# A hybrid decoder layer: the loads behind the weight sums, one token sum's place, and the queue of one transfer

## The chip, the cores and the metric

The kernel runs on one NeuronCore of one Trainium2 chip. Its engines are TensorE (PE in the profile, with PEld for its weight loads), VectorE (DVE), ScalarE (ACT), GpSimd (POOL) and SyncE (SP). The metric is the device time of one execution in microseconds (us). It is compared with the kernel before on the same chip.

## The reference

One layer (DEPTH = 1) works on 256 tokens of width 2048, in float32:

```python
h = rmsnorm(x, norm_mix_g)
u = h @ w_in                       # 2048 x 16384: c, b, xa, za, q, f, iv, og, ga, gb
ya = b * causal_dwconv3(c * xa, conv_w) * silu(za)
yb = per-head rmsnorm(chunked gated recurrence of q, f, iv) * hg_norm_g * silu(og)
m = sigmoid(ga) * (ya @ w_a_out) + sigmoid(gb) * (yb @ w_b_out)
x = x + m @ w_o
gate = sigmoid(rmsnorm(x, ple_norm_g) @ w_ple_gate)
x = x + gate * (p @ w_ple_proj)
out = rmsnorm(x, final_norm_g)
```

## The kernel before, in words

**Three products for one.** Each float32 operand of a large matmul is cut into a high part, which ScalarE writes (`cut`, L169, tiles named ...hi), and a low part, which VectorE writes as the rest (L170, ...lo). TensorE then multiplies three times into the same PSUM bank: high with high (L1038), low with high (L1039), high with low (L1040). The weights come in as raw tiles, `raw[128, 2, 1024]`, which SyncE's queue loads one MB at a time into three buffers (`load`, L150). Each holds two items. One item is 256 rows of the weight matrix by 512 columns and costs twelve matmuls of 128x512; its high and low parts have four buffers.

**The order of the work.** A list `items` gives all items in order, and the loop over `pos` walks through it. At each position it cuts the item three places ahead, multiplies the item at hand, starts loads up to four further ahead, and advances generators (`active`) that hold the epilogues: each `yield` in an epilogue is one position of the loop. The instructions of each engine then stand in an order that a scheduler settles, apart from a stretch (`pinned`) where the traced order is kept. Every queue and engine works its own instructions in order, so one that waits holds up those behind it.

**Seven products for eight.** For the groups j = 1, 2, 3 of the gates ga and gb, five of the eight items (`SEVEN`, c = 0, 2, 3, 5, 6, kind "S") are done with seven block products in place of eight. This needs sums of weight blocks and sums of token blocks. `token_sums` makes the sums of token blocks once, four for each such c (s1 to s4), cuts them and keeps them as `shi`, `slo` in the pool `st`. `combine_weights` makes the sums of weight blocks for each of the fifteen units, two positions ahead. It takes three tiles: `sA` and `sB`, plain loads on SyncE's queue in two buffers each, and `sT`, in three buffers. `sT` is itself a sum, built by two transfers on GpSimd's queue (`add_by_dma`): a plain load (L157), then a second transfer that adds two more blocks to it on its way in (L163). The second waits until the first has landed. The first three pairs are issued at positions fixed by `begun`; every later pair is issued when a unit has been combined. `unit_products` does the seven products of a unit; the block product with the weights `bhi`, `blo` (one buffer) goes third.

**The merged quarters.** `ep_bb` (L778 on) merges the two branches to one quarter of m, 128x1024. Three quarters wait in DRAM. The last one (j = 3) is turned at once: `turned` writes it to DRAM in four transfers (L304), reads it back with another (L315) on SyncE's queue, lets `lag` positions pass, transposes it on VectorE (L308, `back<-t`) and cuts it (`put_m`: L775 on ScalarE, L776 on VectorE) into the operand `mh`, `ml` of the product with `w_o`. That product needs the last quarter only from its seventh item on. The scheduler has put the first item of the next group of columns ahead of this seventh item.

Lines of the steps below: L141 loads of sA and sB; L150 raw loads; L157 and L163 the two transfers of sT; L169 and L170 the cuts; L701 the sums of weights; L760, L762, L763 the sums of tokens and their cut; L308, L315, L775, L776 the way back of the last quarter; L993 and L997 loads of x for the residual and of the final gain.

Of the kernel before, what the change touches and what calls it, by code (L numbers as in the profile page):

```python
# [9 lines left out]
F32 = mybir.dt.float32  # L10
F32R = mybir.dt.float32r
AF = mybir.ActivationFunctionType
ALU = mybir.AluOpType
PSUM = bass.MemoryType.PSUM

P = 128
# [7 lines left out]
CW = 512  # L24
# [7 lines left out]
SEVEN = [()] + 3 * [(0, 2, 3, 5, 6)]  # L32
# [15 lines left out]
def hybrid_kernel(ctx, tc, xT, x, pT, prm, gfin, masks, w_in, w_a, w_b, w_o, w_pg, w_pp, out):  # L48
    nc = tc.nc
# [9 lines left out]
    pools, closers = {}, {}  # L59
# [13 lines left out]
    state = {"tmp": "tmp1"}  # L73
# [3 lines left out]
    def nm(s):  # L77
        uid[0] += 1
        return f"{s}_{uid[0]}"
# [16 lines left out]
    pair_sums = {}  # L96
# [9 lines left out]
    items = []  # L106
# [16 lines left out]
    def raw_of(pos):  # L123
        it = items[pos]
        if it["raw"] not in loaded:
            if it["kind"] == "S":
                t = tuple(
                    pools["st"].tile([P, n, CW], F32, tag=tag, bufs=2, name=nm(tag)) for tag, n in (("sA", 2), ("sB", 1))
                )
            else:  # L130
                t = wp.tile([P, 2, 2 * CW], F32, tag="raw", bufs=3, name=nm("raw"))
            loaded[it["raw"]] = t
        return loaded[it["raw"]]
# [18 lines left out]
    def add_by_dma(behind=None):  # L152
        pos = next((n for n, it in enumerate(items) if it["kind"] == "S" and n not in pair_sums), None)
        if pos is not None:
            w, g, c = items[pos]["w"]
            X = pair_sums[pos] = pools["st"].tile([P, 2, CW], F32, tag="sT", bufs=3, name=nm("sT"))
            d = nc.gpsimd.dma_start(out=X.rearrange("p n x -> p (n x)"), in_=w[g + 1, :, c, :])  # L157
            if behind is not None:
                tc.add_manual_dep(
                    d.ins, behind.name,  # L160
                    mybir.DependencyInfo(mybir.DependencyClass.Sync, mybir.DependencyReason.DATA), reason="order",
                )
            nc.gpsimd.dma_start(out=X, in_=w[g : g + 2, :, c, :CW].rearrange("n p x -> p n x"), accum_op=ALU.add)  # L163

    def pair_of(pool, n, tags=("whi", "wlo"), width=2 * CW):
        return tuple(pool.tile([P, width], F32R, tag=tag, bufs=n, name=nm(tag)) for tag in tags)
# [18 lines left out]
    def combine_weights(pos):  # L185
        st = pools["st"]
        (A, B), X = raw_of(pos), pair_sums[pos]
        add(A[:, 0], X[:, 0], B[:, 0])
        add(A[:, 1], A[:, 0], A[:, 1])
        ts = []  # L190
        for n, src in enumerate((X, B, A)):
            hi, lo = pair_of(st, 1, ("bhi", "blo"), CW) if n == 1 else pair_of(st, 3, ("thi", "tlo"))
# [9 lines left out]
    begun = next(n for n, it in enumerate(items) if it["kind"] == "ga" and it["last"])  # L202
# [7 lines left out]
    prm_t = const.tile([P, PRM_N], F32, name="prm_t")  # L210
    praw = pools["tmp1"].tile([P, 1024], F32, tag="X", bufs=4, name="praw")[:, : 2 * T]
    pop = pools["tmp1"].tile([P, 1024], F32R, tag="X", bufs=4, name="pop")
# [87 lines left out]
    def to_dram(src, tag, bufs):  # L300
        d = dram.tile([P, 4, T], F32, tag=tag, bufs=bufs, name=nm(tag))
        to = d.rearrange("(b i) a x -> a i b x", b=4)
        for a in range(4):
            nc.sync.dma_start(out=to[a], in_=src[32 * a : 32 * a + 32, :].rearrange("i (b x) -> i b x", b=4))  # L304
        return d

    def square_turn(dst, src):
        nc.vector.transpose(  # L308
            out=dst.rearrange("p (k a e) -> p a k e", a=4, e=32), in_=src.rearrange("p (a k e) -> p a k e", a=4, e=32)
        )  # L310

    def turned(src, lag, dst=None):
        d = to_dram(src, "turn", 3)
        yield
        nc.sync.dma_start(out=src, in_=d.rearrange("p a x -> p (a x)"))  # L315
        for _ in range(lag):
            yield
        dst = t4() if dst is None else dst
        square_turn(dst, src)
        return dst  # L320
# [379 lines left out]
    def add(out, a, b):  # L700
        nc.vector.tensor_tensor(out=out, in0=a, in1=b, op=ALU.add)  # L701
# [32 lines left out]

    def token_sums():
        nu = len(SEVEN[1])
        state["S"] = pair_of(pools["st"], 1, ("shi", "slo"), nu * 4 * P)
        state["S"] = tuple(v.rearrange("p (u s t) -> p u s t", u=nu, s=4) for v in state["S"])
        yield
        yield  # L740
        for first, n in TOGETHER:
            yield
            F, S = (
                pools["st"].tile([P, 2 * CW], F32R, tag=tag, bufs=3, name=nm(tag))[:, : n * 4 * P].bitcast(F32)
                for tag in ("thi", "tlo")
            )
            c = SEVEN[1][first]
            hi, lo = (v[:, 2 * c : 2 * (c + n), :] for v in state["hT"])
            Fv = F.rearrange("p (k t) -> p k t", t=T)
            nc.vector.tensor_tensor(out=Fv, in0=hi.bitcast(F32), in1=lo.bitcast(F32), op=ALU.add)  # L750
            yield
            Fv = F.rearrange("p (u r b t) -> p u r b t", u=n, r=2, b=2)
            Sv = S.rearrange("p (u s t) -> p u s t", u=n, s=4)
            a11, a12, a21, a22 = Fv[:, :, 0, 0], Fv[:, :, 1, 0], Fv[:, :, 0, 1], Fv[:, :, 1, 1]
            s1, s2, s3, s4 = (Sv[:, :, i] for i in range(4))
            for out, u, v, op in (
                (s1, a21, a22, ALU.subtract), (s2, s1, a11, ALU.subtract),
                (s3, a11, a21, ALU.subtract), (s4, a12, s2, ALU.add),
            ):
                nc.vector.tensor_tensor(out=out, in0=u, in1=v, op=op)  # L760
            hi, lo = (v[:, first : first + n] for v in state["S"])
            nc.scalar.activation(out=hi, in_=Sv, func=AF.Copy)  # L762
            nc.vector.tensor_tensor(out=lo, in0=Sv, in1=hi.bitcast(F32), op=ALU.subtract)  # L763
            yield

    def ep_a(j, psum):
# [11 lines left out]
    def ep_bb(j, psum):  # L778
        ga, gb = state["ga"], state["gb"]
        for t in range(NT):  # L780
            s = slice(t * CW, (t + 1) * CW)
            nc.vector.tensor_tensor(out=gb[:, s], in0=gb[:, s], in1=psum[t], op=ALU.mult)
        m = t4()
        for t in range(NT):
            s = slice(t * CW, (t + 1) * CW)
            nc.vector.tensor_tensor(out=spread(m, t), in0=blocks(ga[:, s]), in1=blocks(gb[:, s]), op=ALU.add)
        if j == 3:
            m = yield from turned(m, 3, back())
            put_m(j, m)
        else:  # L790
            state["m", j] = to_dram(m, f"m{j}", 1)
            yield

    def back():
        return pools["back"].tile([P, 1024], F32, tag="back", bufs=5, name=nm("back"))
# [259 lines left out]
    def names_of(it):  # L1055
        if it["kind"] == "C":
            return [("c", it["n"], t) for i in range(2) for t in range(NT)]
        return ["P1", ("c", 0, 0), ("c", 1, 0), "P5", "P7", "P6", ("c", 0, 1)]

    def into(name, op, part):  # L1060
        left[name] -= 1
# [3 lines left out]
    def unit_products(pos):  # L1065
        it = items[pos]
        c, h = it["c"], state["hT"]

        def x_of(r, t):
            return tuple(v[:, 2 * c + r, t * P : (t + 1) * P] for v in h)  # L1070

        hi, lo = parts.pop(pos)
        halves = [(hi[:, i * CW : (i + 1) * CW], lo[:, i * CW : (i + 1) * CW]) for i in range(2)]
        names = names_of(it)
        if it["kind"] == "C":
            for n, name in enumerate(names):
                into(name, x_of(n // 2, n % 2), halves[n // 2])
            return
        b22, t1, t3, t2, t4_ = sums.pop(pos)
        s1, s2, s3, s4 = (tuple(v[:, SEVEN[1].index(c), i] for v in state["S"]) for i in range(4))  # L1080
        for name, op, part in zip(names, (x_of(0, 0), x_of(1, 0), s4, s1, s3, s2, x_of(1, 1)),
                                  (halves[0], halves[1], b22, t1, t3, t2, t4_)):
            into(name, op, part)

    def pinned(start):
# [16 lines left out]
    for pos, it in enumerate(items[:last_group]):  # L1102
        mark = len(nc.cur_bb.bb.instructions)
        kind, j, c, last = (it[n] for n in ("kind", "j", "c", "last"))
        _, _, w, g, opname = groups[it["gi"]]
# [60 lines left out]
        else:  # L1166
            if c == 0:
                psum = [bank("s" if kind == "PP" and j >= 2 else "g") for _ in range(NT)]
            hi, lo = parts.pop(pos)
            for i in range(2):  # L1170
                k = 2 * c + i
                s = slice(i * CW, (i + 1) * CW)
# [10 lines left out]
        if pos == begun:  # L1183
            finish()
            second_part()
            active.append(token_sums())
        if pos in (begun + 3, begun + 5, begun + 7):
            add_by_dma(state["splits"][0])
        if kind == "O" and j == 0 and c == nch - 3:
            finish()  # L1190
# [23 lines left out]
    for t, halves in ((0, (0, 1)), (1, (0,)), (1, (1,))):  # L1214
        bk, n = bank("g"), CW // 2
        for c in range(nlast):
# [3 lines left out]
            hi, lo = parts[last_group + c]  # L1220
            for i in range(2):
                k = 2 * c + i
                s = slice(i * CW + halves[0] * n, i * CW + (halves[-1] + 1) * n)
# [83 lines left out]
```

## Time and profile before

| | |
|---|---|
| time, median of 3 runs (lowest to highest) | 817.6 us (816.24 to 818.68) |
| the profiled execution: time, span | 816.5 us, 814.7 us |
| granted TensorE clock | 0.996 of full speed |
| busy: PE, PEld, DVE, ACT, POOL | 803.2, 665.4, 589.2, 459.4, 48.5 us |
| moved by DMA | 198.52 MB, mean 244 GB/s |

The span runs from the first instruction to the last. The time of an execution holds the span and what lies around it, here 1.8 us. All positions below, such as "at 473.0", are us from the start of the span.

### The profile page before, as it was taken

The numbers are of one execution on the slowest core, as the hardware profiler recorded it, in microseconds if no ns is written. First come the engines' busy times: TensorE is split into PE (matmuls) and PEld (weight loads), VectorE is DVE, ScalarE is ACT, GpSimd is POOL, SyncE is SP. The second block draws the span as 40 slices with busy tenths as digits, with TensorE's granted clock in tenths as the row PEclk, the third lists the DMA queues.
The fourth block names the chain that finished last, engine by engine and source line by source line (L and its number), as shares of the span: only waits on it lengthen the run. The fifth ranks groups of instructions, "written<-read, shape, count | busy, mean of one in ns | idle before, by whom it ended". The sixth has DMA issues, their size and how long they took to land.

```text
span 814.7 us, 10651 instructions
## 1 busy us (share of the span) xinstructions
PE 803.2 (99%) x4059; PEld 665.4 (82%) x4059; DVE 589.2 (72%) x745; ACT 459.4 (56%) x614; POOL 48.5 (6%) x57
## 2 busy tenths in 40 slices
PE   9999999999999999999999999999999999999995
PEld 6888888888888888888888878888888788888885
DVE  7746588767766498767679968987988756677932
ACT  7576476466565466456455546556554546566623
POOL 1000000001000000010011110110100000001210
PEclk9999999999999999999999999999999999999998
DMA  9988555648867555648789989998944888777802
GB/s 339 392 307 288 197 201 175 233 139 267 252 237 249 198 175 196 207 157 269 259 296 282 286 268 297 284 280 260 283 163 177 291 300 300 255 274 298 276 34 103
DMA packets 52659, 198.52 MB, mean 244 GB/s; under 512 B 6784, under 2 KB 16256, under 8 KB 37888
## 3 DMA queue, kind: packets, MB, share of 16 engines
q1 hardware_dynamic: 45504, 180.54, 63.6%
q0 software_dynamic: 6240, 15.73, 8.2%
q10 hardware_dynamic: 864, 1.57, 0.5%
q8 instruction: 31, 0.51, 0.2%
q14 instruction: 20, 0.16, 0.1%
HBM read 184.19 MB, written 13.63 MB: 243 GB/s over the span
## 4 chain that ended last, share of the span: by engine, by line
PE 85%; DVE 7%; issue 4%; DMA 2%; ACT 2%; POOL 0%; POOLq 0%; DVEq 0%; ACTq 0%
PE g L1038 26%; PE g L1039 26%; PE g L1040 25%; DVE wlo L170 3%; PE s L1039 2%; PE s L1040 2%; PE s L1038 2%; DMA sT<-in_w_in 1%; DMA raw<-in_w_o 1%; PE s L484 1%; DVE sA L701 1%; ACT whi L169 0%; DVE tlo L170 0%; PE s L932 0%; DVE back L308 0%
## 5 line engine op out<-in xcount | busy, mean ns | idle before, releaser
L170 DVE TENSOR_TENSOR wlo<-raw,whi 128x1024 fp32r<-128x1024 f32 (+1 forms) x264 | 319.9, 1229 | 159.9 <-ACT whi L169 158.0
L169 ACT ACTIVATE whi<-raw 128x1024 fp32r<-128x1024 f32 (+1 forms) x264 | 272.9, 1051 | 208.1 <-PE g L1040 175.2
L1038 PE MATMUL g<-whi,xh 128*128 128x512 f32 (+1 forms) x738 | 283.8, 385 | 0.0
L1039 PE MATMUL g<-wlo,xh 128*128 128x512 f32 (+1 forms) x738 | 283.7, 384 | 0.0
L1040 PE MATMUL g<-whi,xl 128*128 128x512 f32 (+1 forms) x738 | 283.6, 384 | 0.0
L1040 PEld LDWEIGHTS g<-whi,xl 128*128 128x128 f32 x738 | 138.7, 188 | 27.8
L1038 PEld LDWEIGHTS g<-whi,xh 128*128 128x128 f32 x738 | 138.7, 188 | 27.5
L1039 PEld LDWEIGHTS g<-wlo,xh 128*128 128x128 f32 x738 | 138.7, 188 | 27.1
L1039 PE MATMUL g<-wlo,mh 128*128 128x512 f32 x128 | 49.9, 390 | 0.3 <-DVE wlo L170 0.3
L1038 PE MATMUL g<-whi,mh 128*128 128x512 f32 x128 | 49.6, 389 | 0.0
L1040 PE MATMUL g<-whi,ml 128*128 128x512 f32 x128 | 49.5, 389 | 0.0
L1040 PE MATMUL s<-whi,xl 128*128 128x512 f32 x84 | 32.7, 389 | 0.0
L1038 PE MATMUL s<-whi,xh 128*128 128x512 f32 x84 | 32.7, 389 | 0.0
L1039 PE MATMUL s<-wlo,xh 128*128 128x512 f32 x84 | 32.7, 389 | 0.0
L169 ACT ACTIVATE thi<-sA 128x1024 fp32r<-128x1024 f32 x15 | 15.9, 1063 | 25.0 <-DVE sA L701 21.3
L1039 PEld LDWEIGHTS g<-wlo,mh 128*128 128x128 f32 x128 | 24.0, 188 | 5.6 <-DVE wlo L170 0.7
L1038 PEld LDWEIGHTS g<-whi,mh 128*128 128x128 f32 x128 | 24.0, 188 | 5.1
L1040 PEld LDWEIGHTS g<-whi,ml 128*128 128x128 f32 x128 | 24.0, 188 | 5.0
L1039 PE MATMUL g<-wlo,ybTh 128*128 128x512 f32 x64 | 24.9, 389 | 0.0
L1040 PE MATMUL g<-whi,ybTl 128*128 128x512 f32 x64 | 24.9, 389 | 0.0
L1038 PE MATMUL g<-whi,yaTh 128*128 128x512 f32 x64 | 24.9, 389 | 0.0
L1039 PE MATMUL g<-wlo,yaTh 128*128 128x512 f32 x64 | 24.9, 389 | 0.0
(215 smaller groups left out, 910.2 us busy)
## 6 DMA issues: line engine op xcount, KB each, us to landing
raw<-in_w_in SPq DMA_DIRECT2D x66, 1024.0 KB, 5.0
raw<-in_w_o SPq DMA_DIRECT2D x16, 1024.0 KB, 6.1
raw<-in_w_pg SPq DMA_DIRECT2D x16, 1024.0 KB, 5.7
sT<-in_w_in POOLq DMA_DIRECT2D x30, 512.0 KB, 8.5
raw<-in_w_in SPq DMA_DIRECT2D x28, 512.0 KB, 6.9
raw<-in_w_a SPq DMA_DIRECT2D x8, 1024.0 KB, 6.4
raw<-in_w_b SPq DMA_DIRECT2D x8, 1024.0 KB, 7.7
turn<-t SPq DMA_DIRECT2D x60, 128.0 KB, 2.8
```

Of the source, the lines that this page charges most:

```text
L169: a = nc.scalar.activation(out=hi, in_=src, func=AF.Copy)
L170: v = nc.vector.tensor_tensor(out=lo, in0=src, in1=hi.bitcast(F32), op=ALU.subtract)
L484: nc.tensor.matmul(out, X[:, 0, h, s], X[:, 1, h, t], start=True, stop=True, tile_position=(0, i * n))
L701: nc.vector.tensor_tensor(out=out, in0=a, in1=b, op=ALU.add)
L1038: nc.tensor.matmul(psum, oh, hi, start=first, stop=False)
L1039: nc.tensor.matmul(psum, oh, lo, start=False, stop=False)
L1040: nc.tensor.matmul(psum, ol, hi, start=False, stop=last)
```

## The change

`sT` gets a fourth buffer and `sB` a third. The plain load of a unit's `sT` is now issued before the accumulating transfer of the unit before it, and a fourth call starts the series, so plain loads run one unit further ahead. Of the four token sums, the fourth (s4) no longer stands in `shi`, `slo`: it takes the place of a block of x that no later product reads, in `xh`, `xl`. Each of the three cuts of token sums becomes two for this, and the product that uses s4 (with `bhi`, `blo`) goes first in its unit instead of third. The last merged quarter is read back on GpSimd's queue, with a lag of 5.

```diff
-                    pools["st"].tile([P, n, CW], F32, tag=tag, bufs=2, name=nm(tag)) for tag, n in (("sA", 2), ("sB", 1))
+                    pools["st"].tile([P, n, CW], F32, tag=tag, bufs=bufs, name=nm(tag))
+                    for tag, n, bufs in (("sA", 2, 2), ("sB", 1, 3))
...
-            X = pair_sums[pos] = pools["st"].tile([P, 2, CW], F32, tag="sT", bufs=3, name=nm("sT"))
+            X = pair_sums[pos] = pools["st"].tile([P, 2, CW], F32, tag="sT", bufs=4, name=nm("sT"))
             d = nc.gpsimd.dma_start(out=X.rearrange("p n x -> p (n x)"), in_=w[g + 1, :, c, :])
...
-            nc.gpsimd.dma_start(out=X, in_=w[g : g + 2, :, c, :CW].rearrange("n p x -> p n x"), accum_op=ALU.add)
+        if "adding" in state:
+            w, g, c = items[state["adding"]]["w"]
+            X = pair_sums[state.pop("adding")]
+            with tc.issue_after(d.ins) if pos is not None else ExitStack():
+                nc.gpsimd.dma_start(
+                    out=X, in_=w[g : g + 2, :, c, :CW].rearrange("n p x -> p n x"), accum_op=ALU.add
+                )
+        if pos is not None:
+            state["adding"] = pos
...
-    def turned(src, lag, dst=None):
+    def turned(src, lag, dst=None, queue=nc.sync):
...
-        nc.sync.dma_start(out=src, in_=d.rearrange("p a x -> p (a x)"))
+        queue.dma_start(out=src, in_=d.rearrange("p a x -> p (a x)"))
...
-        state["S"] = pair_of(pools["st"], 1, ("shi", "slo"), nu * 4 * P)
+        state["S"] = pair_of(pools["st"], 1, ("shi", "slo"), nu * 3 * P)
...
-            hi, lo = (v[:, first : first + n] for v in state["S"])
-            nc.scalar.activation(out=hi, in_=Sv, func=AF.Copy)
-            nc.vector.tensor_tensor(out=lo, in0=Sv, in1=hi.bitcast(F32), op=ALU.subtract)
+            sums_of = tuple(v[:, first : first + n] for v in state["S"])
+            fourth = tuple(v[:, 2 * c : 2 * (c + n) : 2, P:] for v in state["hT"])
+            for (hi, lo), src in ((sums_of, Sv[:, :, :3]), (fourth, Sv[:, :, 3])):
+                nc.scalar.activation(out=hi, in_=src, func=AF.Copy)
+                nc.vector.tensor_tensor(out=lo, in0=src, in1=hi.bitcast(F32), op=ALU.subtract)
...
-            m = yield from turned(m, 3, back())
+            m = yield from turned(m, 5, back(), nc.gpsimd)
...
-        return ["P1", ("c", 0, 0), ("c", 1, 0), "P5", "P7", "P6", ("c", 0, 1)]
+        return [("c", 1, 0), "P1", ("c", 0, 0), "P5", "P7", "P6", ("c", 0, 1)]
...
-        if pos in (begun + 3, begun + 5, begun + 7):
+        if pos in (begun + 3, begun + 5, begun + 7, begun + 9):
             add_by_dma(state["splits"][0])
```

More of the change, by code (lines that the diff above doesn't have):

```diff
@@ L736, in token_sums @@
         nu = len(SEVEN[1])
-        state["S"] = pair_of(pools["st"], 1, ("shi", "slo"), nu * 4 * P)
-        state["S"] = tuple(v.rearrange("p (u s t) -> p u s t", u=nu, s=4) for v in state["S"])
+        state["S"] = pair_of(pools["st"], 1, ("shi", "slo"), nu * 3 * P)
+        state["S"] = tuple(v.rearrange("p (u s t) -> p u s t", u=nu, s=3) for v in state["S"])
         yield
@@ L1079, in unit_products @@
         b22, t1, t3, t2, t4_ = sums.pop(pos)
-        s1, s2, s3, s4 = (tuple(v[:, SEVEN[1].index(c), i] for v in state["S"]) for i in range(4))
-        for name, op, part in zip(names, (x_of(0, 0), x_of(1, 0), s4, s1, s3, s2, x_of(1, 1)),
-                                  (halves[0], halves[1], b22, t1, t3, t2, t4_)):
+        s1, s2, s3 = (tuple(v[:, SEVEN[1].index(c), i] for v in state["S"]) for i in range(3))
+        s4 = x_of(0, 1)
+        for name, op, part in zip(names, (s4, x_of(0, 0), x_of(1, 0), s1, s3, s2, x_of(1, 1)),
+                                  (b22, halves[0], halves[1], t1, t3, t2, t4_)):
             into(name, op, part)
```

## The prediction

> **What bounds the kernel now.** I read the page's busy times first, then the waits of PE, then the time windows. The waits' columns are total, times, longest.
>
> ```profile
> PE 803.2 (99%) x4059; PEld 665.4 (82%) x4059; DVE 589.2 (72%) x745; ACT 459.4 (56%) x614; POOL 48.5 (6%) x57
> ...
> PE s L932 <- DVE warm L928: 1.5, 1, 1.5
> PE s L1039 <- DVE blo L170: 1.0, 1, 1.0
> PE g L1039 <- DVE wlo L170: 0.3, 1, 0.3
> ...
> 440.00:460.00 20.00, 20.00 (x90) 16.58 (x89) 19.55 (x24) 11.85 (x13) 3.56 (x4) 1.00 1.02 315
> 460.00:480.00 20.00, 18.95 (x84) 15.34 (x84) 15.42 (x17) 11.74 (x14) 3.55 (x4) 1.00 0.77 209
> 640.00:660.00 20.00, 19.71 (x87) 15.95 (x87) 12.98 (x13) 10.10 (x13) 0.00 (x0) 1.00 0.93 331
> ```
>
> PE is busy for 803.2 of 814.7 us. Its first wait (1.5) is the start, and the tail follows its last product; the change touches neither. Between them lie two waits: 1.04 us (window 460 to 480) and 0.29 us (640 to 660). Counted from start to start, as products overlap, they cost somewhat more: 1.33 and 0.57, worked out below. The number of products does not change, so only these 1.9 us can be won from this execution, 0.23%. About 0.3%, 2.45 us, is what a measurement of this kernel can tell from no change. What can be lost is not so limited.
>
> **Part one: the wait at 476.** It belongs to the fifth unit. The fence holds GpSimd's queue, the landing of the transfer issued at 461.51, then the engines; the last two landings are the longest of an accumulating transfer (issued at 540.3) and of a plain one behind it (541.1).
>
> ```profile
> 442.23 0.59 POOL L157 DMA_DIRECT2D sT<-in_w_in  x1 [0.81 <-DVE tlo L170]
> 452.36 0.59 POOL L157 DMA_DIRECT2D sT<-in_w_in  x1 [1.38 <-DVE tlo L170]
> 461.51 1.18 POOL L163 DMA_DIRECT2D sT<-in_w_in  x1 [8.56 <-DMA sT<-in_w_in]
> ...
> sT<-in_w_in POOLq DMA_DIRECT2D x1, 512.0 KB, 11.3
> ...
> 457.44 0.69 DVE L170 TENSOR_TENSOR blo<-sB,bhi 128x512 fp32r<-128x512 f32 x1
> 467.32 1.22 DVE L170 TENSOR_TENSOR wlo<-sA,whi 128x1024 fp32r<-128x1024 f32 x1
> 473.02 0.69 DVE L701 TENSOR_TENSOR sA<-sT,sB 128x512 f32<-128x512 f32 x1 [4.48 <-DMA sT<-in_w_in]
> 475.49 0.68 DVE L170 TENSOR_TENSOR blo<-sB,bhi 128x512 fp32r<-128x512 f32 x1
> ...
> 457.79 0.39 PE L1038 MATMUL g<-thi,xh 128*128 128x512 f32 x1
> 459.82 0.39 PE L1038 MATMUL s<-bhi,shi 128*128 128x512 f32 x1
> 474.79 0.39 PE L1038 MATMUL s<-bhi,shi 128*128 128x512 f32 x1
> 476.23 0.50 PE L1039 MATMUL s<-blo,shi 128*128 128x512 f32 x1 [1.04 <-DVE blo L170]
> 476.80 0.39 PE L1038 MATMUL g<-thi,shi 128*128 128x512 f32 x1
> ...
> sT<-in_w_in POOLq DMA_DIRECT2D x1, 512.0 KB, 12.6
> sT<-in_w_in POOLq DMA_DIRECT2D x2, 512.0 KB, 12.9
> ```
>
> The plain load at 452.36 waited for a buffer (VectorE's cut of the second unit); the accumulation could follow only when it had landed, at 461.51, and took 11.3 us to 472.8. VectorE, free from 468.54, waited 4.48 us, and `blo` was done at 476.17, 3.15 us after the sum's start. Products start every 0.226 us (nine from 457.79 to 459.82), so PE wanted `blo` at 475.02. The product at 476.80 is the third after that of 474.79 and was due at 475.47: the wait costs 1.33 us, the 1.04 shown and a slow restart.
>
> With four buffers the load of the fifth unit takes the one that came free at 442.23, ten us sooner. If it lands as badly as any, 12.9 us later, its accumulation goes at 455.1 and lands at 467.7 by the worst 12.6. In GpSimd's queue it stands behind the load of the sixth unit, which waits for the buffer freed at 452.36; that comes earlier. The product with `blo` now goes first in its unit, six products or 1.36 us sooner than 475.02, at 473.66; the sum must start by 470.5. So 467.7 leaves 2.8 us, and VectorE at 468.54 leaves 2.0. **Gain: 1.33 us.** No other unit loses: each accumulation waits for a buffer three units back instead of for its own late load.
>
> The same move of `blo` costs margin elsewhere. The tightest is the third unit: `blo` done at 458.13, wanted until now at 459.82 + 0.23, from now on at 458.69. 0.56 us are left; cost 0.
>
> **Part two: the token sums.** Three cuts on ScalarE and three on VectorE become six each.
>
> ```profile
> 432.42 1.06 ACT L762 ACTIVATE shi<-tlo 128x1024 fp32r<-128x1024 f32 x1 [3.91 <-DVE tlo L760]
> ...
> 415.02 0.69 DVE L763 TENSOR_TENSOR slo<-tlo,shi 128x512 fp32r<-128x512 f32 x1 [0.70 <-ACT shi L762]
> 433.51 1.23 DVE L763 TENSOR_TENSOR slo<-tlo,shi 128x1024 fp32r<-128x1024 f32 x1 [1.13 <-ACT shi L762]
> ```
>
> A split adds one fixed part: 2 x 0.69 - 1.23 = 0.15 us on VectorE, 0.45 in all. VectorE stands idle for 1.13 us before its cut, waiting for ScalarE, whose first piece now is a quarter shorter (0.26 us). So VectorE starts 0.26 earlier and does 0.15 more: cost 0. Without that cover it would be 0.45 late at the third unit, still inside the 0.56.
>
> **Part three: the way back of the last quarter.** The rows are SyncE's queue and the landing of the transfer at 642.84, then the engines; then the three plain `sT` loads that found GpSimd's queue empty or nearly (407.6, 503.98, 565.87), and what SyncE issued around the first.
>
> ```profile
> 642.84 0.34 SPq L315 DMA_DIRECT2D t<-turn  x1
> 643.27 1.01 SPq L150 DMA_DIRECT2D raw<-in_w_o  x2
> ...
> t<-turn SPq DMA_DIRECT2D x1, 512.0 KB, 4.1
> ...
> 646.84 0.61 PE L1038 MATMUL g<-whi,mh 128*128 128x512 f32 x2
> 648.31 0.39 PE L1039 MATMUL g<-wlo,mh 128*128 128x512 f32 x1
> 647.60 1.24 DVE L308 STREAM_TRANSPOSE back<-t 128x1024 f32<-128x1024 f32 x1
> 648.88 1.07 ACT L775 ACTIVATE mh<-back 128x1024 fp32r<-128x1024 f32 x1 [0.78 <-DVE back L308]
> 650.15 0.40 PE L1038 MATMUL g<-whi,mh 128*128 128x512 f32 x1
> ...
> sT<-in_w_in POOLq DMA_DIRECT2D x1, 512.0 KB, 8.5
> sT<-in_w_in POOLq DMA_DIRECT2D x1, 512.0 KB, 5.0
> sT<-in_w_in POOLq DMA_DIRECT2D x1, 512.0 KB, 4.7
> ...
> 406.68 2.60 SPq L150 DMA_DIRECT2D raw<-in_w_a  x2
> ```
>
> The quarter lands at 646.94, VectorE's transpose starts at 647.60 in its turn, `mh` is done at 649.95, and PE starts the first product that reads it at 650.15. This chain has 0.2 us in hand, and PE shows no wait only because it is met. In the built program the transpose, the cuts and the products keep their places whatever the lag of 5 says, so PE waits as soon as the landing passes 650.15 - 2.35 = 647.80, that is 4.96 us after the issue at 642.84, and pays a restart (1.33 against 475.02 to 476.17, 0.2 us) on top. GpSimd's queue issues at the same moment: it waits for the same four pieces and has nothing else. A plain load of this size took 4.7, 5.0 and 8.5 us there, so PE loses 0 to 3.7 us. The 8.5 had MB-sized raw loads beside it, as this place has, the other two only smaller ones; I take the mean, 6.1, **a loss of 1.3 us**. VectorE's next cut stands behind the transpose; PE, late by the same amount, needs it later still. Just before lies the wait of 0.29: five products in a row start at 646.84, the last at 648.31 instead of 647.74, 0.57 us. Its raw load, ahead of the read-back, stays where it is: no gain taken, 0.57 at most.
>
> The Trainium skill speaks against this part: "DMA: Bandwidth & Descriptors", sections "Issuing engine by pattern" and "SWDGE vs HWDGE vs iDMA", sends plain transfers to SyncE or ScalarE as the generally faster path. The rows agree: 4.1 us against at best 4.7.
>
> **SyncE's queue.** It loses the read-back, so the two raw loads behind it at 643.27 go earlier; nobody waits for them. In the built program two loads of x and the 1 MB gain now stand ahead of raw loads, 1.57 MB.
>
> ```profile
> 655.88 0.33 SPq L150 DMA_DIRECT2D raw<-in_w_o  x1
> ...
> raw<-in_w_o SPq DMA_DIRECT2D x16, 1024.0 KB, 6.1
> ...
> 666.68 1.06 ACT L169 ACTIVATE whi<-raw 128x1024 fp32r<-128x1024 f32 x1 [1.66 <-PE g L1040]
> ```
>
> At the window's 331 GB/s that is 4.75 us. The raw load of 655.88 lands near 662 and is cut at 666.68, held by PE alone; PE needs the item three items (36 products, 8.2 us) later, less about 2.3 for the cuts. 4.7 + 5.9 = 10.6 us hide 4.75: cost 0, and without cover up to 4.75.
>
> **The sum.** 816.5 - 1.3 + 1.3 = 816.5 for an execution like the profiled one. That one lies 1.1 below the median of the three runs, so the median stays 817.6: no change that a measurement can tell.
>
> **The rivals.**
> - *The return is in time* (landing within about 5.5 us; 4.7 and 5.0 speak for it, 8.5 against). Net -1.9 (with the other wait gone as well) to -0.6: 815.7 to 817.0. The same page's section "Anatomy of one DMA" gives a GpSimd transfer 2.0 us plus its bytes at 436 GB/s, an estimate of 3.2 us here; by it the time would be 816.3, but no row of this size is below 4.7.
> - *Slower: the return lands late.* From 8.6 us on the loss passes 3.8 and the net 2.45. The 8.5 under raw loads speaks for it, the two others against: 820.1 at 8.6.
> - *SyncE's order uncovers a raw load or a turned quarter*: decides only past the 10.6 us of cover; 817.6 - 1.3 + 4.75 = 821.0 at most.
> - *The other runs of before hold more of these waits than the profiled one* (the three differ by 2.4 us, and both chains hang on landings that vary from 4.7 to 12.9): with all of them gone the median falls to 814.6 (816.5 - 1.9) or 814.3, 1.9 below the lowest.
> - *The change doesn't do it*: the accumulation, now behind a load that waits for a buffer, comes late again. That needs the buffer after 457.9, 5.5 later than seen: 817.6 + 1.3 = 818.9.
>
> **How the numbers follow.** Return late by less than that 0.39 (net -0.6 to +2.4, 817.0 to 820.0), in time 0.25, still waiting 0.03, late enough to be slower 0.12, SyncE's order 0.05, the runs of before 0.16. That gives faster 0.16, within 0.3% 0.67, slower 0.17. The range reaches from 814.6 to 820.4 (820.1 and 0.3 us beside it).
>
> **What would show it.** Right: no wait of PE for `blo`; GpSimd's accumulations issued without waits of 8 us for landings; a wait of PE on `mh` (or ScalarE's cut behind a transpose that waits for the turned quarter) near 649, as long as the landing on GpSimd's queue exceeds 4.96. Wrong: PE busy 99% with the way back landing under 5 us, a new wait for a raw tile between 655 and 690, or a first `blo` late in a unit.

## The result, and the profile after

The changed kernel is slower: 820.05 us median (818.71 to 823.7, 12 executions) against 816.67 us (814.8 to 819.77, 12 executions) for the kernel before on the same chip. The ratio is 1.0044, 95% interval 1.0028 to 1.006, so 3.6 us, 2.3 to 4.9. The profiled execution took 820.75 us with a span of 818.7, 4.0 us more than the span of the one profiled before.

The first fence is from the page and from the waits of PE (total, times, longest).

```profile
PE 804.8 (98%) x4059; PEld 665.8 (81%) x4059; DVE 590.2 (72%) x748; ACT 458.6 (56%) x617; POOL 48.8 (6%) x58
...
PE g L1049 <- ACT mh L786: 2.4, 1, 2.4
PE s L943 <- DVE warm L939: 1.5, 1, 1.5
PE g L1049 <- ACT whi L178: 0.8, 2, 0.5
PE g L1050 <- DVE wlo L179: 0.5, 1, 0.5
```

The wait for `blo` is gone. A wait of 2.4 us for `mh`, the last merged quarter, stands in its place, and the waits for the raw tile ahead of it (`whi` and `wlo`, one of the `whi` waits being the kernel's start) have grown. Time windows of the two stretches, with PE's busy time first and the granted clock, DMA share and GB/s last:

```profile
440.00:480.00 40.00, 40.00 (x179) 33.10 (x178) 37.16 (x42) 23.65 (x26) 8.99 (x10) 1.00 1.00 302
...
650.00:652.00 2.00, 0.00 (x0) 0.00 (x0) 2.00 (x2) 0.75 (x1) 0.00 (x0) 1.00 0.02 8
652.00:654.00 2.00, 1.65 (x5) 1.33 (x6) 1.98 (x3) 1.26 (x2) 0.00 (x0) 0.69 0.89 212
654.00:656.00 2.00, 2.00 (x6) 1.59 (x5) 0.69 (x1) 0.00 (x0) 0.00 (x0) 0.50 0.94 218
656.00:658.00 2.00, 2.00 (x10) 1.58 (x9) 0.00 (x0) 0.53 (x1) 0.00 (x0) 0.96 0.85 345
```

In the 40 us that held the first wait, PE now has none. In the second stretch two things show. PE stands still from before 650 to 652.36, and after that it is busy but at half its clock: 6 products in the two microseconds from 654, where 9 or 10 are usual. The busy share alone would have hidden this second loss.

The way of the last quarter, in the timeline and in the landing of the transfer issued at 641.85:

```profile
637.84 14.84 SPq L151 DMA_DIRECT2D raw<-in_w_o  x4
...
641.85 0.57 POOL L324 DMA_DIRECT2D t<-turn  x1 [71.14 <-DMA turn<-t]
...
t<-turn POOLq DMA_DIRECT2D x1, 512.0 KB, 8.1
...
645.02 2.01 ACT L178 ACTIVATE whi<-raw 128x1024 fp32r<-128x1024 f32 x2 [3.69 <-DMA raw<-in_w_o]
651.25 1.06 ACT L786 ACTIVATE mh<-back 128x1024 fp32r<-128x1024 f32 x1 [4.21 <-DVE back L317]
...
649.97 1.25 DVE L317 STREAM_TRANSPOSE back<-t 128x1024 f32<-128x1024 f32 x1 [2.63 <-DMA t<-turn]
...
649.57 0.39 PE L1051 MATMUL g<-whi,ml 128*128 128x512 f32 x1
652.36 0.50 PE L1049 MATMUL g<-whi,mh 128*128 128x512 f32 x1 [2.39 <-ACT mh L786]
...
653.50 0.63 PE L1050 MATMUL g<-wlo,mh 128*128 128x512 f32 x1
653.92 0.63 PE L1049 MATMUL g<-whi,mh 128*128 128x512 f32 x1
...
656.34 0.40 PE L1051 MATMUL g<-whi,ml 128*128 128x512 f32 x1
```

The read-back landed after 8.1 us, where it took 4.1 on SyncE's queue. The product with `mh` started at 652.36 instead of 649.80 (0.23 after that of 649.57): 2.56 us. The ten steps from there to 656.34 took 3.98 us instead of 2.27: 1.71 us. And SyncE, which before had stood between the first and the second raw load until the four pieces were written, no longer stands there: the first raw load is issued at 637.84 and the second 1.5 us later, where before it came 4.1 us later. The first of them landed after 7.1 us, against 6.1 before, and ScalarE cut it from 645.02.

PE's order is the same in all kernels here outside single units, so its records can be set side by side by number. The stages below are the start of the 500th product, the times from there to the 2900th, on to the 3400th and on to the last one, and from it to the end of the span (us):

| kernel | to 500th | to 2900th | to 3400th | to the last | to the end | span |
|---|---|---|---|---|---|---|
| before | 116.81 | 435.71 | 113.96 | 139.23 | 9.00 | 814.7 |
| after | 116.80 | 434.36 | 119.29 | 139.23 | 9.04 | 818.7 |
| after - before | 0.0 | -1.35 | +5.33 | 0.00 | 0.0 | +4.0 |

The whole change of the profiled execution lies in two stages: parts one and two gain 1.35, the stretch with the read-back loses 5.33 (raw tile 0.98, late start 2.56, half clock and restart the rest).

### The profile page after: what moved, and what is told of

The parts are those of the page before. It is cut to its first block, busy times and chain, and to the rows that moved or that the text cites. A ratio compares the mean times of both kernels' runs of the same rounds, so it can differ in the third digit from the quotient of the medians.

```text
span 818.7 us, 10658 instructions
## 1 busy us (share of the span) xinstructions
PE 804.8 (98%) x4059; PEld 665.8 (81%) x4059; DVE 590.2 (72%) x748; ACT 458.6 (56%) x617; POOL 48.8 (6%) x58
## 4 chain that ended last, share of the span: by engine, by line
PE 90%; DVE 3%; issue 2%; DMA 2%; ACT 2%; SPq 0%; POOLq 0%; POOL 0%
PE g L1049 27%; PE g L1051 27%; PE g L1050 27%; PE s L1051 3%; PE s L1050 3%; PE s L1049 3%; DVE wlo L179 2%; DMA t<-turn 1%; DVE back L317 1%; PE s L493 1%; ACT mh L786 1%; DMA turn<-t 0%; DMA praw<-in_pT 0%; ACT whi L178 0%; PE s L594 0%
```

## The experiments

Theory A: the read-back on GpSimd's queue (part three) holds the whole loss; parts one and two gain. Its rival puts part of the loss into the other two parts. Two further theories differ in why the read-back is late: a slowness of GpSimd's queue (Q), or company, because on another queue the transfer no longer stands in line between the raw loads but shares the transfer engines with them (C).

**Each half alone.** First the changed kernel with the read-back on SyncE's queue again, and the lag of 3 that belongs to it:

```diff
-            m = yield from turned(m, 5, back(), nc.gpsimd)
+            m = yield from turned(m, 3, back())
```

> Parts one and two with the read-back of the last merged quarter on SyncE's queue again (lag 3). Theory A, the whole loss lies in the read-back on GpSimd's queue: the wait for blo stays gone (1.33 us), the read-back lands some 4 us after its issue, PE does not wait for mh, the two waits for the raw tile before it (0.8 and 0.5 in the changed kernel) shrink to the 0.29 of before, and the time is about 1.3 us below the kernel before (ratio 0.998). Theory B, part of the loss comes with the loads put ahead or the token sums: the waits for the raw tile near 646 stay at 0.8 and 0.5, and the time is that of the kernel before or up to 1 us above it (ratio 1.000 to 1.001).

815.46 us, ratio 0.9993 (0.9984 to 1.0002). Its list of waits holds the start alone, and its read-back landed in 3.6 us:

```profile
PE s L943 <- DVE warm L939: 1.5, 1, 1.5
...
t<-turn SPq DMA_DIRECT2D x1, 512.0 KB, 3.6
```

Then the kernel before with part three alone (the same line and the `queue` argument of `turned`):

> The kernel before with part three alone: the read-back of the last merged quarter on GpSimd's queue, lag 5. Theory A: landing about 8 us, PE waits some 2.4 us for mh and then multiplies at half clock for some 3.5 us, the raw tile ahead comes 1 us later; the wait for blo (1.33) is still there: 5 us above the kernel before (ratio 1.006 to 1.007). Theory B: 3 to 4 us above it (ratio 1.004 to 1.005), the rest of the changed kernel's loss being in the other parts.

822.64 us, ratio 1.0081 (1.0068 to 1.0093).

```profile
PE g L1038 <- ACT mh L775: 2.4, 1, 2.4
...
PE s L1039 <- DVE blo L170: 1.2, 1, 1.2
...
654.00:656.00 2.00, 1.61 (x7) 1.35 (x8) 1.98 (x3) 1.29 (x2) 0.00 (x0) 1.00 0.86 196
```

So A holds: without part three nothing is lost, and part three alone loses more than the changed kernel does. The last row holds a surprise. This execution waited as long for `mh`, and PE's clock stayed at 1.00 behind it. Its other timed executions had a mean clock of 0.993 against 0.996 here and spans of 820.0 to 821.1 against 819.2: the half clock comes in some executions and not in others.

**Why the read-back is late: another queue, and no company.** The read-back on ScalarE's queue:

```diff
-            m = yield from turned(m, 5, back(), nc.gpsimd)
+            m = yield from turned(m, 5, back(), nc.scalar)
```

> The changed kernel with the read-back on ScalarE's queue in place of GpSimd's. Theory Q, a transfer on GpSimd's queue is slow by itself: it lands here within 4 to 5 us as on SyncE's queue, PE waits for mh 0.3 us at most, the time is 1 us below the kernel before. Theory C, the read-back is slow on any queue beside that of the raw loads, because it no longer stands between them but shares the transfer engines with them: it lands after 7 to 8 us, PE waits 1.5 to 2.5 us, the time is 2.5 to 3.5 us above the kernel before.

820.19 us, ratio 1.0055 (1.0042 to 1.0068); PE waits longer than in the changed kernel, as the landing is later still, beyond what either theory expected:

```profile
PE g L1049 <- ACT mh L786: 2.9, 1, 2.9
...
t<-turn ACTq DMA_DIRECT2D x1, 512.0 KB, 8.9
```

Q falls: ScalarE's queue, which issues the transfer in 0.33 us where GpSimd's takes 0.57, lands it no sooner. The test from the other side leaves the read-back on GpSimd's queue and keeps the raw loads away. A small transfer on SyncE's queue reads from the landed quarter, and the second and later raw loads are ordered behind it:

```diff
         queue.dma_start(out=src, in_=d.rearrange("p a x -> p (a x)"))
+        if hold:
+            probe = dram.tile([P, 8], F32, tag="probe", bufs=1, name="probe")
+            state["probe"] = nc.sync.dma_start(out=probe, in_=src[:, :8]).ins
...
+            with tc.issue_after(state["probe"]) if new and state["held"] > 1 else ExitStack():
+                load(q)
```

> The changed kernel, but a 4 KB transfer on SyncE's queue that reads the turned quarter stands between the first raw load behind the four pieces and the second: SyncE sends no further raw load until the read-back on GpSimd's queue has landed. Theory C, the read-back is slow because raw loads share the transfer engines with it: it now lands 4 to 5.5 us after its issue, PE waits for mh under 0.5 us, and the first raw tile is cut in time (wait 0.3 us as before the change). Theory Q, GpSimd's queue has a slowness of its own beside that: it still lands after 6 us or more. The second raw load goes some 5 us later than in the kernel before, so a new wait of PE of up to 4 us for its tile may follow; the time says nothing here.

> The kernel in which SyncE sends no further raw load until the read-back has landed on GpSimd's queue, now timed. By its one profile the landing takes 3.8 us, PE does not wait for mh, and the raw tile behind it comes late by 1.3 us of waits; parts one and two gain 0.5 to 1.3. Theory C: ratio 0.999 to 1.0015, no execution with a clock under 0.996. Rival, that one profile was a lucky landing: the ratio is 1.003 or more.

The first profile (one execution, 815.98 us) gave 3.8 us and no wait for `mh`. Timed, the same kernel took 815.22 us, ratio 0.9995 (0.9987 to 1.0004), all eleven clocks at 0.996 or 0.997, and landed in 3.8 us again:

```profile
637.47 0.39 SPq L151 DMA_DIRECT2D raw<-in_w_o  x1
645.26 0.34 SPq L327 DMA_DIRECT2D probe<-t  x1
645.69 8.86 SPq L151 DMA_DIRECT2D raw<-in_w_o  x4
...
t<-turn POOLq DMA_DIRECT2D x1, 512.0 KB, 3.8
```

SyncE sends one raw load, then nothing until the quarter has landed. GpSimd's queue is then as quick as SyncE's (4.1 before, 3.6 in the first experiment), and the loss is gone. C holds, and as the lag is 5 here, the lag is not the cause. For the held raw loads PE did not wait at all, where I had allowed up to 4 us. (The 1.3 us of waits that I expected again at the raw tile were misread: 1.05 of them lie at the kernel's start; the raw tile ahead of the quarter cost 0.25 us in the first profile and 0.2 in the second.)

**How much company.** Two attempts to start the read-back level with the second raw load came out otherwise. In the first, the small transfer read from the first of the four pieces only, so SyncE did not stand until all were written: the second raw load's instruction started 1.5 us behind the first one's, as in the changed kernel, and only took longer (0.97 us instead of 0.35):

```diff
+            state["probe"] = nc.sync.dma_start(out=probe, in_=d[:, 0, :8]).ins
```

> The changed kernel, but a 4 KB transfer on SyncE's queue that reads the four written pieces stands where the read-back stood before the change: SyncE sends the second raw load only once the pieces are written, as in the kernel before. This gives back SyncE's hold and leaves the read-back on GpSimd's queue, at the same moment as the second raw load. Theory D, the wait for the first raw tile (0.8 and 0.5 in the changed kernel, 0.29 before) grew because the second raw load runs beside the first: it is 0.3 us here. The read-back itself, now beside raw loads that start when it does, lands after 6 to 8 us and PE waits 1 to 2.4 us for mh. Rival: the first raw tile is as late as in the changed kernel, its lateness being that of the landing of the pieces or of chance.

One execution, 822.04 us. The first raw load landed in 5.8 us and PE did not wait for its tile; the read-back took 7.9, PE waited 3.5 us for `mh` and ran at a mean clock of 0.66 in the ten microseconds from 650.

The second attempt read two elements from every row and piece (`d[:, :, :2]`), 512 packets of 8 bytes:

> As the run before with the small transfer on SyncE's queue, but it reads from all four written pieces, so that SyncE sends the second raw load at the very moment of the read-back on GpSimd's queue, as in the kernel before; nothing waits for the landing. Theory B, the read-back is slow because the raw loads' packets already stand in line when it starts (a backlog of up to 2 MB in the changed kernel): it now starts level with one load and lands in 4.5 to 6 us, PE waits 0 to 1 us, the time is within 1.5 us of the kernel before. Theory S, sharing alone does it, whoever started first: it lands after 7 to 8 us, PE waits 2.5 to 3.5 us, the time is 4 to 6 us above the kernel before.

821.54 us, ratio 1.0073 (1.0061 to 1.0086); landing 8.9 us. It reads as theory S (sharing alone makes the read-back late), but the small packets had a price of their own: the first raw load took 7.9 us. Nothing follows for the read-back. With 16 packets of 256 bytes (`d[:1]`, one row of all four pieces) the order is the intended one:

> As the run with the small transfer that reads from all four pieces, but it reads 4 KB in one stretch, 16 packets of 256 B, in place of 512 packets of 8 B, which had themselves disturbed the queues (the first raw load took 8.0 us there, against 5.8 to 6.2 in all other runs in which no second raw load followed at once). SyncE's order is that of the kernel before; the read-back on GpSimd's queue starts level with the second raw load. Theory B, a backlog of raw packets is what slows the read-back: it lands in 4.5 to 6 us and PE waits 0 to 1 us for mh, time within 1.5 us of the kernel before. Theory S, sharing alone does it: it lands after 7 to 9 us, PE waits 2.4 to 3.5 us, time 3.5 to 6 us above the kernel before. Theory D on the first raw tile: its load lands after 5.8 to 6.2 us again and PE's wait for it is at most 0.5 us.

818.02 us, ratio 1.0028 (1.0017 to 1.0039).

```profile
641.31 0.57 SPq L328 DMA_DIRECT2D probe<-turn  x1
641.98 8.99 SPq L151 DMA_DIRECT2D raw<-in_w_o  x3
...
t<-turn POOLq DMA_DIRECT2D x1, 512.0 KB, 6.4
...
PE g L1053 <- ACT mh L790: 1.8, 1, 1.8
```

The result lies between B (a backlog of raw loads does it) and S: 6.4 us, a wait of 1.8. So both count. With nothing beside it but the end of the first raw load the transfer takes 3.8 us, started level with the second raw load 6.4, behind two raw loads already under way 7.9 to 8.9. In its old place in SyncE's line it took 3.6 to 4.1, as it stood ahead of those loads. The traces' packets show the two parts: the read-back's first packet starts 1.3 us after the issue with the loads held and also here, but 3.1 in the changed kernel, and its last one 3.3, 5.6 and 7.2 us after the issue. The backlog holds up the start by 1.8 us; sharing stretches what follows.

The first raw load landed in 6.0 us here. It takes 5.9 to 6.2 us in the seven profiles in which SyncE stands behind it until the four pieces are written, and 6.4 to 7.1 in five in which the second load follows 1.5 us behind. That speaks for theory D, but it is not shown: two profiles do not fit, the one with the 8-byte packets (7.9) and the first attempt above, whose second load also started 1.5 us behind and whose first one took 5.8.

**The clock.** Ten products into a bank that nobody reads, meant to fill the wait:

```diff
+            if kind == "O" and j == 0 and c == 6:
+                spare = bank("s")
+                for _ in range(10):
+                    nc.tensor.matmul(spare, hi[:, :P], hi[:, :CW], start=True, stop=True)
```

> The changed kernel with ten more products of 128x512, into a bank that nobody reads, on PE between the last product before the wait for mh and the first one after it: 2.3 us of work in a wait of 2.4. Theory H, PE's clock is halved because PE stood still: with the gap filled the granted clock stays near 1.00 after it, the products that follow start every 0.23 us, and the time is 1.7 us below the changed kernel (ratio to before about 1.002). Rival: the products after the wait are slow for another reason, such as late cuts or the transfers beside them; they still start every 0.43 us, and the time is that of the changed kernel (ratio 1.004) or up to 2.3 us above it.

820.27 us, ratio 1.0052 (1.0038 to 1.0066). The fillers ran twelve products too early, beside the wait for the raw tile, and left a wait of 1.7 us for `mh`; clocks from 0.995 to 0.998. In a second form they were ordered directly ahead of the first product that reads `mh`:

> The changed kernel with ten products of 128x512 into a bank that nobody reads, now held on PE directly ahead of the first product that reads mh (in the first filled kernel they came twelve products too early and left 1.7 us of the wait). They take 2.3 us of a wait of 2.4 and so cost nothing by themselves. Theory H, PE's standing still is what lowers its clock: no execution shows a granted clock under 0.996, the products behind the wait start every 0.23 us, and the time is that of the changed kernel's executions at full clock, 3 us above the kernel before (ratio 1.003 to 1.004). Rival, the clock falls for another reason: part of the executions show 0.993 to 0.995 as in the changed kernel, and the ratio is 1.0044 to 1.006.

819.72 us, ratio 1.0048 (1.0035 to 1.0061), clocks 0.995 once and 0.996 four times. The landing was later still in the profiled one, the execution with 0.995:

```profile
649.42 2.43 PE L1192 MATMUL s<-wlo 128*128 128x512 f32 x10
653.20 0.50 PE L1049 MATMUL g<-whi,mh 128*128 128x512 f32 x1 [1.35 <-ACT mh L786]
...
t<-turn POOLq DMA_DIRECT2D x1, 512.0 KB, 8.6
```

Theory H wanted no execution below 0.996, and one is: the fillers covered the first 2.3 us of a longer wait, and the 1.35 us that were left, with a wait of 0.53 close behind, were enough to lower the clock. H is therefore not shown by this experiment. What speaks for it is the set of all timed executions, and then the clock records of the traces. Where the read-back lands in time (the first experiment and the held one, 22 executions) every clock is 0.996 or 0.997. With the late read-back it spreads. In the changed kernel:

| mean granted clock | spans of its executions, us |
|---|---|
| 0.996 to 0.997 | 816.9, 817.1, 817.3, 817.5, 817.7, 818.1 |
| 0.995 | 818.4, 818.7, 818.8, 819.3 |
| 0.993 | 820.7, 820.8 |

From the first row to the last the clock falls by 0.004, which over 818 us is 3.3 us, about what the spans differ by.

Why it falls in one execution and not in another can be read from the traces' clock records. In each of the five profiles with a fall ahead of the last product, that fall and the one behind the last product lie a whole multiple of 3.41 us apart (in the changed kernel 652.74 and 813.17, 47 times). Laid from there backwards, a grid of 3.41 us divides each trace, and what counts is how long PE stood still within one interval:

| profile | PE still in the fullest interval, us | clock in the next one |
|---|---|---|
| fillers, second form | 1.87 | 0.50 |
| part two alone | 1.92 | 0.50 |
| changed kernel | 2.39 | 0.50 |
| 8-byte packets | 2.41 | 0.50 |
| small transfer from the first piece | 2.67 | 0.50 |
| fillers, first form | 1.69 | 1.00 |
| read-back on ScalarE's queue | 1.63 (wait of 2.87, the other 1.24 in the next) | 1.00 |
| part three alone | 1.54 (wait of 2.40, the other 0.85 in the one before) | 1.00 |

In the other six profiles no interval behind the kernel's start and ahead of its last product holds more than 1.24 us, and the clock stays at 1.00. So in all fourteen profiles the clock falls exactly where PE stood still long enough within one interval, and whether a wait of 2 to 3 us is enough depends on where the grid cuts it. An interval at half clock costs half its length, 1.7 us. This is read from the traces; no run here moved a wait on the grid on purpose.

**Part two alone, and the kernel before once more.** Part two alone is the kernel before with the hunks of `token_sums`, `names_of` and `unit_products`:

```diff
-        return ["P1", ("c", 0, 0), ("c", 1, 0), "P5", "P7", "P6", ("c", 0, 1)]
+        return [("c", 1, 0), "P1", ("c", 0, 0), "P5", "P7", "P6", ("c", 0, 1)]
```

> The kernel before with part two alone: the fourth token sum in the place of a block of x, its cuts split, its product first in the unit. By the prediction's step the splits cost nothing, but the product with blo now comes 1.36 us sooner while the sum of weights comes no sooner: the wait for blo in the fifth unit grows from 1.04 to about 2.4 us and the time is 1 to 1.4 us above the kernel before (ratio 1.0015). Rival: the wait is a matter of chance of that one execution, and the time is that of the kernel before (ratio 0.9995 to 1.0005).

817.65 us (814.57 to 820.78), ratio 1.0012 (0.9996 to 1.0029): undecided, with executions on both sides. Its profile shows the wait that the new order asks for, and a lowered clock behind it:

```profile
PE s L1041 <- DVE blo L170: 1.2, 1, 1.2
PE s L1040 <- ACT bhi L169: 0.8, 1, 0.8
...
460.00:480.00 20.00, 18.08 (x72) 14.28 (x71) 15.59 (x17) 10.75 (x13) 3.55 (x4) 0.91 0.76 207
```

A unit whose first product needs `bhi` and `blo` must have its sums sooner; part one is what provides that.

> The kernel before once more, for a second profile. If the waits of PE for blo (1.04) and for the raw tile (0.29) come in every execution, both are here again within 0.3 us; if they hang on how long single transfers took, one of them is gone or twice as long, and the gain of parts one and two over a typical execution is smaller than the 1.6 us read from the profiles.

816.33 us, span 814.6. Its waits in the two places are not those of the first profile:

```profile
PE g L1039 <- DVE wlo L170: 0.4, 1, 0.4
PE s L1039 <- DVE blo L170: 0.2, 1, 0.2
```

The stages of these profiles, as above:

| kernel | to 500th | to 2900th | to 3400th |
|---|---|---|---|
| before, second profile | 117.31 | 434.89 | 114.13 |
| parts one and two | 116.72 | 434.38 | 113.77 |
| part three alone | 116.73 | 436.52 | 117.59 |
| part two alone | 116.62 | 438.50 | 114.03 |
| read-back on ScalarE's queue | 117.27 | 434.68 | 117.91 |
| raw loads held | 116.44 | 434.36 | 113.81 |
| level start | 116.69 | 434.41 | 115.99 |

The wait for `blo` cost 1.35 us in one profile of the kernel before and 0.5 in the other, against 434.37 in the kernels with parts one and two. Part three alone, which is the kernel before in this stage, lost 2.15 there. All the kernels of both tables take 139.23 us from the 3400th product to the last.

## Why the prediction was wrong, step by step

I forecast no measurable change at 817.6 us; it became slower by 3.6 us, past the bound of 2.45. The measured 820.05 lies inside the range that I gave, but at the end that only the slower rivals reached.

*What bounds the kernel.* Right: PE's waits account for every difference, apart from the clock behind them, which the view of waits does not show.

*Part one.* The mechanism was right, and so was the size for that execution: 1.33 us predicted, 1.35 read. But a wait that hangs on a landing was taken from one profile as if it came every time. The second profile holds 0.5, that of part three alone 2.15, and parts one and two together gain 0.6 us by the ratio, anywhere from 1.3 gained to 0.2 lost. The rival by which other executions of the kernel before hold more of these waits is not borne out: of these two one holds more and one less. One reading was off without effect: the row of 12.9 is the median of two landings, 12.6 and 13.2, so the worst case left 2.5 us of margin, not 2.8.

*Part two.* Cost 0 was right beside part one: 434.38 us with it and no wait. It is not free by itself, as the wait for `bhi` and `blo` shows.

*Part three, the step that failed.* I allowed the landing 4.96 us from the issue and set its price by three plain loads on GpSimd's queue, 4.7, 5.0 and 8.5. I wrote that the 8.5 had raw loads beside it "as this place has", and then took the mean, 6.1. The right value was the one from the like situation: 7.9 to 8.9 in every kernel that left the raw loads alone. The term of 1.3 became 2.56 for the late start.

*SyncE's queue, the second step that failed.* I wrote of "the two raw loads behind it at 643.27" that they "go earlier; nobody waits for them." Nobody waits for them, but the read-back pays, which loses its place ahead of them, and in this profile PE also started on the first raw tile 0.98 us later; that this second loss comes from the early loads is likely, not shown. I took it that SyncE's wait could go at no cost, and it was what kept the way clear.

*A term that was missing: the clock.* For the restart I took 0.2 us from the wait of 1.04; behind the wait of 2.39 the half clock and the restart cost 1.71 in the profiled execution. Behind the like wait of part three alone, where the clock stayed, the six steps from 654.39 to 655.88 lost 0.1.

*SyncE's order from 655 on.* Right: 139.23 us to the last product in every profile of the two tables, so the loads of x and of the gain cost nothing.

*The rivals.* The slower one was the mechanism that came, with a chance of 0.12 and a threshold of 8.6 us. The threshold was too high because the raw tile and the clock were not in it: 8.1 was enough. The sum with the measured terms is -1.35 + 0.98 + 2.56 + 1.71 = +3.9, for a span longer by 4.0.

*The rule of the Trainium skill* that I weighed ("DMA: Bandwidth & Descriptors", "Issuing engine by pattern") pointed the right way for a reason that the runs do not show: GpSimd's queue took 3.8 us alone, ScalarE's 8.9 in company. The rule that bears on the loss stands on the same page under "Issuing engines are not separate DMA queues": transfers of all issuing engines run on the same DMA engines and interleave. The landings of 3.8, 6.4 and 7.9 to 8.9 agree with it.

## What to carry to other kernels

A transfer that a critical chain waits for has a place in its queue, and moving it to an idle queue gives that place up: it then shares with everything the old queue sends, and the old queue, no longer held by its wait, sends more. Price such a move from a transfer of the same size with the same company, not from a mean over quiet and busy moments. And where new waits on TensorE come to about 2 us close together, look at the granted clock in the windows behind them before believing the length of the wait.

## What the runs showed of the hardware

The clock fell to one half behind a wait of 2.4 us, and for 3.41 us (products every 0.43 us from 652.7 to 656.1), but not in each execution: a wait of 2.40 on the kernel before with part three and one of 2.9 with ScalarE's queue left it at 1.00 in their profiles, while 1.2 and 0.8 us close together lowered it in the one with part two. In these fourteen profiles it fell where PE stood still for 1.87 us or more within one interval of a fixed grid of 3.41 us, and not at 1.69 or less. The Trainium skill, "TensorE: Matmul & The Clock Gate", section "Part 1: The HAM clock gate", describes a gate with two states, half and full, that closes after an idle window of about 3.4 us and opens after a busy one, on a window that runs freely. The half, the 3.41 us and the grid agree; that the clock can fall when PE stood still for only 1.87 of the 3.41 us differs, and here the runs decide.

In one profile each, a transfer of 4 KB in 512 pieces of 8 bytes delayed a 1 MB load that had been issued 3.6 us earlier, from about 6 us to 7.9; the same 4 KB in 16 pieces did not (6.0).
